# A decoder layer on Trainium2: the last expert taken out of the normalisation of all tokens, its tokens normalised by slots and scattered

## Chip, core and metric

The kernel runs on one core of one Trainium2 chip. The metric is the device time of one execution in microseconds; lower is better. Before the change it is 1770.06 us, the median of 3 runs (1768.85 to 1771.56).

## What is computed

One decoder layer over 256 tokens of width 2048, in float32: a mixer of retention and gated linear attention, cross-attention into 256 memory tokens, and a mixture of 32 experts of which each token takes two. Each of the three is followed by `x <- LayerNorm(alpha * x + f(x))`. The change touches only the end of the third:

```python
    hid = jax.nn.silu(xblk @ w_exp_gate[e]) * (xblk @ w_exp_up[e])
    return hid @ w_exp_down[e]
...
    h = layer_norm(DEEPNORM_ALPHA * h + ffn, ln3_g[l], ln3_b[l])
...
    y = (xf - mu) * lax.rsqrt(var + LN_EPS) * g.astype(jnp.float32) + b.astype(jnp.float32)
```

`ffn` adds, for each token, its two experts' outputs times their gates.

## The kernel before

**Experts.** Each expert has 32 slots (`CAP`). `gather` (by a 0/1 matrix on TensorE) brings the tokens of four experts into slots; `gate_up(e)` multiplies them with the expert's gate and up weights, which come in four quarters of 2 MB (`gu`, line 1082), each used by two of the eight rounds of its loop; SiLU, product and transposes give `hht`; `down_all(e, hht)` multiplies with the down weights, two halves of 2 MB (`dp`, line 1120). One expert's output is 32 slots x 2048 values; in PSUM it stands as 128 partitions x 512, four column blocks of 512 under each other. `combine` brings the outputs of four experts back to the tokens: a matmul with the transposed, gate-weighted slot matrix `GT` (line 1513) and an addition into `fo` (line 1515), the sum `alpha * h + ffn` of all 256 tokens, in two halves of 128 tokens.

**Order of the work.** Each engine runs its instructions in the order in which the code is written. Small background steps (generators in `bgq`) are put between the rounds of `gate_up` by `step()`: `combine`, and for the last LayerNorm `bg_gb3` (line 1461, put in at expert 29), which loads gamma and beta of `ln3` as rows (`raw3`, line 1468), splits them into `row3` for a matmul of 6 rows, and spreads gamma and beta over all partitions (`gb3`, line 1482, from `row_bcast`, line 1446).

**Transfers.** All weights are loaded by SyncE (SP) in one queue, in the order of use, each as soon as its buffer is free: gate/up quarters and other large tiles share one pool of 8 buffers, the down halves a pool of 3. SP's transfers report to eight semaphores, `DMAHW0` to `DMAHW7`, in turn; a transfer waits until the one eight places ahead of it has landed.

**The last expert (31).** Its down weights are stored apart (`w_last`), cut by columns (`LASTC`: three blocks of 512 columns and two of 256). For each block `down(i)` multiplies, ScalarE copies the slots out (`ys`, line 1624), and `finish(i - 1)` brings the block before to all tokens (line 1631), adds it (1632), takes the block's statistics (`bn_stats`, 1635), and GpSimd multiplies it by gamma (1638). Then `ln_rstd` (841 to 843) gives mean and 1/std, lines 1649 to 1657 turn them into `nbT`, and each block of 512 columns is finished by a matmul of 6 rows and one VectorE instruction (1674, 1675) and stored (1660); the last 512 columns go another way (1664 to 1669).

Of the kernel before, what the change touches and what calls it, by code (L numbers as in the profile page):

```python
# [36 lines left out]
MOX = [0, 0, 1, 0, 0, 1, 9, 9]  # L37


LASTC = [(0, 512), (512, 512), (1024, 512), (1536, 256), (1792, 256)]  # L40


def bcast_rows(ap1d, n, off=0, parts=128):
# [4 lines left out]
def layer(ctx: ExitStack, tc: tile.TileContext, a, out):  # L48
# [1075 lines left out]
    lastw = []  # L1124

    def dn_cols(c0, n):

        def load():
            if c0 % 1024 == 0:
                lastw.append(qq[0].tile([128, 4 * 1024], F32, name="dl", tag="q"))  # L1130
            c = c0 % 1024
            t = lastw[-1][:, 4 * c:4 * c + 4 * n]
            sp.dma_start(out=t, in_=a["w_last"][:, 4 * c0:4 * c0 + 4 * n])
            t = t.rearrange("p (k f) -> p k f", k=4)
            return [t[:, k] for k in range(4)]
        return xpiece(load, "q", int(c0 % 1024 == 0))
# [324 lines left out]

    def bg_gb3():
        g_, r_ = pair([128, 2, D], name="gb3"), pair([6, 2, D], name="raw3")
        gb3.extend(g_[:, i] for i in range(2))
        raw, hi, r3 = r_[:, 0], r_[:, 1].bitcast(F32R), single([6, D], F32R, name="row3")
        gb3.append(r3)
        for i, k, n in ((0, 4, "ln3_g"), (4, 2, "ln3_b")):
            sp.dma_start(out=raw[i:i + k], in_=bcast_rows(a[n][0], D, parts=k))
        yield True

        odd = s1("odd", (6, 4))
        oi = odd[:, 0:1].bitcast(I32)
        dve.tensor_scalar(oi, pi[:6, 1, 0:1], 1, None, op0=OP.bitwise_and)
        dve.tensor_copy(odd[:, 1:2], oi)
        dve.tensor_scalar(odd[:, 2:3], odd[:, 1:2], -2.0, 1.0, op0=OP.mult, op1=OP.add)
        act.activation(hi, raw, AF.Copy)  # L1476
        act.activation(raw, raw, AF.Copy, scale=odd[:, 1:2])
        dve.scalar_tensor_tensor(r3, hi.bitcast(F32), odd[:, 2:3], raw, op0=OP.mult, op1=OP.add)
        yield True
        for c in range(4):  # L1480
            for i in range(2):
                act.activation(gb3[i][:, c * 512:c * 512 + 512], row_bcast(2 + i, c), AF.Copy)
            yield True


# [122 lines left out]
    drain()  # L1608


    g3, b3, row3 = gb3
    yq = {}
    nbr = s1("nbr", (128, 2, 6))
    pool.memset(nbr, 1.0)

    def down(i):
        c0, n = LASTC[i]
        py = acc_ps([128, n])
        k = 0
        for w in xtake(dn_ids[i]):  # L1620
            mm(py[32 * k:32 * k + 32], hht[:, 32 * k:32 * k + 32], w, start=True, stop=True)  # L1621
            k += 1
        yq[i] = s2("ys", (128, n))
        act.activation(yq[i], py, AF.Copy)

    def finish(i):
        c0, n = LASTC[i]
        sl = slice(c0, c0 + n)
        for t in range(2):
            p = aux_ps([128, n])  # L1630
            mm(p, GT[(LAST,)][:, t * 128:(t + 1) * 128], yq[i], start=True, stop=True)  # L1631
            dve.tensor_tensor(fo[t][:, sl], fo[t][:, sl], p, op=OP.add)  # L1632
        for t in range(2):
            for c in range(c0, c0 + n, 256):
                dve.bn_stats(lnst[:, t, c // 256], fo[t][:, c:c + 256])  # L1635
        if n == 512:
            for t in range(2):
                pool.tensor_tensor(fo[t][:, sl], fo[t][:, sl], g3[:, sl], op=OP.mult)

    down(0)  # L1640
    for i in range(1, len(LASTC)):
        down(i)
        if i == 4:
            act.activation(lnrs[:, :, 0], lnrs[:, :, 0], AF.Sqrt)
        finish(i - 1)
    finish(len(LASTC) - 1)
    assert xs["loaded"] == len(xpieces)
# [11 lines left out]
    def store(t, sl):
        sp.dma_start(out=out[0, t * 128:(t + 1) * 128, sl], in_=fo[t][:, sl])  # L1660

    sl = slice(1536, D)
    d = fo[1][:, sl]
    act.activation(d, d, AF.Identity, scale=lnrs[:, 1, 1:2], bias=nb[:, 1:2])
    pool.tensor_tensor(d, d, g3[:, sl], op=OP.mult)
    pool.tensor_tensor(d, d, b3[:, sl], op=OP.add)
    d = fo[0][:, sl]
    dve.scalar_tensor_tensor(d, d, lnmv[:, 0, 0:1], g3[:, sl], op0=OP.subtract, op1=OP.mult)
    dve.scalar_tensor_tensor(d, d, lnrs[:, 0, 1:2], b3[:, sl], op0=OP.mult, op1=OP.add)
# [28 lines left out]
def _layout(inputs):  # L1698

    gate, up = (inputs[n][0].reshape(NE, 4, 4, 128, 512) for n in ("w_exp_gate", "w_exp_up"))  # L1700
    last = inputs["w_exp_down"][0][NE - 1].reshape(128, 4, D)
    return {
        "x_T": _rows(inputs["x"][0].T, 0, T, 0, 16).reshape(128, 16, T),
        "mem_T": _rows(inputs["mem"][0].T, 0, T, 0, 16).reshape(128, 16, T),
        "w_gl": _rows(inputs["w_in"][0], 7168, 16, 0, 16).reshape(128, 16, 16),
        "w_last": np.concatenate([last[:, :, c:c + n].reshape(128, 4 * n) for c, n in LASTC], axis=1),
        "w_gu": np.stack([up, gate], axis=2).transpose(0, 1, 4, 2, 3, 5).reshape(NE, 4, 128, 4096),
        "w_dense": np.empty((ND, 128, 1024), np.float32),
    }
# [23 lines left out]
```

## Time and profile before

| | us |
|---|---|
| median of 3 runs | 1770.06 |
| the profiled execution | 1768.08 |
| its span, first to last instruction | 1766.2 |
| TensorE busy | 1486.6 (84%) |
| VectorE, ScalarE, GpSimd busy | 639.9, 546.2, 58.9 |
| mean granted TensorE clock | 0.921 |
| read from HBM | 554.86 MB |

The page divides the span into 40 slices of 44 us. In the first half TensorE is busy in nine tenths or more and the DMA engines in five to eight tenths; from the 23rd slice (about 970 us) the DMA engines are at nine tenths or more, which is the stage of the experts. The views of the trace put every instruction in order of time; a float32 matmul stands there as two records.

### The profile page before, as it was taken

What the parts mean: (1) busy time and instruction counts of PE and PEld (TensorE: products, weight loads), DVE (VectorE), ACT (ScalarE), POOL (GpSimd) and SP (SyncE); (2) the same over time, 40 slices, a digit from 0 to 9 for tenths busy, and PEclk for the clock granted to TensorE, in tenths of its full rate; (3) what the DMA queues carried; (4) which work ended last, traced back from release to release, by engine and by line L of the source; (5) the groups of instructions that cost most, each with busy time, mean ns of one, the idle gap of its engine ahead of it and who ended that gap; (6) DMA issues with size and microseconds to landing.
All of it is one profiled execution on the core that took longest, in us unless ns stands there. A gap on an engine that the chain in (4) does not pass through costs nothing. (4 is left out here: it accounts for less than half of the span.)

```text
span 1766.2 us, 25332 instructions
## 1 busy us (share of the span) xinstructions
PE 1486.6 (84%) x10828; PEld 1000.3 (57%) x10828; DVE 639.9 (36%) x981; ACT 546.2 (31%) x830; POOL 58.9 (3%) x56
## 2 busy tenths in 40 slices
PE   9999999999999999999986776677577657675667
PEld 7788888888888889889542322323123223231332
DVE  6575665665445767555231010010010100100105
ACT  6545444554443565443320201111102011111031
POOL 0000110000000041000000000000000000000002
PEclk9999999999999999999988878887888888888978
DMA  8554555655567655686999999999999999999996
GB/s 266 165 180 155 170 169 201 224 169 189 195 206 218 199 171 180 234 321 252 412 429 429 431 429 432 430 430 430 430 431 430 431 430 430 430 430 432 429 389 248
DMA packets 81665, 558.67 MB, mean 316 GB/s; under 512 B 15046, under 2 KB 15430, under 8 KB 57094
## 3 DMA queue, kind: packets, MB, share of 16 engines
q1 hardware_dynamic: 81548, 556.99, 80.5%
q8 instruction: 87, 1.43, 0.3%
q14 instruction: 30, 0.25, 0.0%
HBM read 554.86 MB, written 2.10 MB: 315 GB/s over the span
## 5 line engine op out<-in xcount | busy, mean ns | idle before, releaser
L1555 PE MATMUL acc<-gu,yz 128*32 128x256 f32 x3584 | 286.9, 466 | 153.8 <-DMA gu<-in_w_gu 148.8
L154 DVE TENSOR_TENSOR wl<-wr,wh 128x1024 fp32r<-128x1024 f32 x271 | 334.8, 1249 | 155.3 <-ACT wh L153 140.8
L153 ACT ACTIVATE wh<-wr 128x1024 fp32r<-128x1024 f32 x271 | 281.8, 1056 | 173.7 <-DMA wr<-in_w_dense 92.3
L1555 PEld LDWEIGHTS acc<-gu,yz 128*32 128x32 f32 x3584 | 118.3, 126 | 330.8 <-DMA gu<-in_w_gu 207.8
L1586 PE MATMUL acc<-dp,eht 128*32 128x512 f32 x944 | 148.0, 758 | 67.8 <-DMA dp<-in_w_exp_down 61.5
L1571 DVE TENSOR_TENSOR ehh<-acc,ehh 64x256 f32<-64x256 f32 x32 | 13.3, 416 | 427.3 <-ACT ehh L1570 427.3
L1592 ACT ACTIVATE yz<-acc 32x512 f32<-32x512 f32 x124 | 72.9, 588 | 208.3 <-PE acc L1586 207.2
L1570 ACT ACTIVATE ehh<-acc 64x256 f32<-64x256 f32 x32 | 12.2, 380 | 363.5 <-PE acc L1555 363.5
L1586 PEld LDWEIGHTS acc<-dp,eht 128*32 128x32 f32 x944 | 30.1, 125 | 154.3 <-DMA dp<-in_w_exp_down 78.1
L1515 DVE TENSOR_TENSOR fo<-fo,aux 128x512 f32<-128x512 f32 x64 | 44.0, 687 | 174.1 <-PE aux L1513 174.1
L208 PE MATMUL acc<-wh,xT 128*128 128x512 f32 x256 | 101.5, 397 | 0.0
L210 PE MATMUL acc<-wh,xT 128*128 128x512 f32 x256 | 99.8, 390 | 0.0
L209 PE MATMUL acc<-wl,xT 128*128 128x512 f32 x256 | 99.7, 389 | 0.0
L229 PE MATMUL acc<-xT,wh 128*128 128x512 f32 x384 | 97.8, 399 | 1.5 <-ACT wh L153 1.2
L229 PEld LDWEIGHTS acc<-xT,wh 128*128 128x128 f32 x384 | 70.2, 190 | 15.5 <-ACT wh L153 1.4
L1316 PEld LDWEIGHTS aux<-P,h 128*128 128x128 f32 x512 | 59.9, 192 | 15.9 <-issue 15.8
L1322 DVE TENSOR_SCALAR yz<-aux,lnT 128x128 f32<-128x128 f32 x56 | 19.1, 403 | 133.8 <-PE aux L1316 133.8
L1513 PE MATMUL aux<-yz,GT 128*128 128x512 f32 (+1 forms) x128 | 66.7, 647 | 0.0
L1316 PE MATMUL aux<-P,h 128*128 128x128 f32 x512 | 66.5, 282 | 0.0
L229 PE MATMUL acc<-h1T,wh 128*128 128x512 f32 x256 | 63.9, 394 | 0.0
L229 PE MATMUL acc<-memT,wh 128*128 128x512 f32 x256 | 63.8, 394 | 0.0
L208 PEld LDWEIGHTS acc<-wh,xT 128*128 128x128 f32 x256 | 48.0, 188 | 10.9 <-issue 1.1
(392 smaller groups left out, 2024.8 us busy)
## 6 DMA issues: line engine op xcount, KB each, us to landing
gu<-in_w_gu SPq DMA_DIRECT2D x127, 2048.0 KB, 27.0
wr<-in_w_dense SPq DMA_DIRECT2D x271, 512.0 KB, 3.4
dp<-in_w_exp_down SPq DMA_DIRECT2D x59, 2048.0 KB, 31.1
dn<-in_w_exp_down SPq DMA_DIRECT2D x8, 512.0 KB, 3.9
dl<-in_w_last SPq DMA_DIRECT2D x3, 1024.0 KB, 28.8
mtok<-in_mem_T SPq DMA_DIRECT2D x2, 1024.0 KB, 6.7
xr<-in_x SPq DMA_DIRECT2D x4, 512.0 KB, 4.3
gu<-in_w_gu SPq DMA_DIRECT2D x4, 512.0 KB, 9.7
```

The lines of the kernel that those rows point to most:

```text
L153: act.activation(hi, raw, AF.Copy)
L154: dve.tensor_tensor(lo, raw, hi.bitcast(F32), op=OP.subtract)
L208: mm(accs[t], xh, hi[:, kc], start=(K == 0), stop=False)
L209: mm(accs[t], xh, lo[:, kc], start=False, stop=False)
L210: mm(accs[t], xl, hi[:, kc], start=False, stop=(K == 15))
L229: mm(accs[f].rearrange("p (a b) -> p a b", a=2), wf, xt, start=(q + kc == 0), stop=(q + kc == 6))
L1316: mm(p[:, k], h2[t][:, (m * q + k) * 128:(m * q + k + 1) * 128], P[:, t], start=(t == 0), stop=(t == 1))
L1513: mm(p, GT[es][:m, t * 128:(t + 1) * 128], y[:m, c * 512:(c + 1) * 512], start=True, stop=True)
L1515: dve.tensor_tensor(d, d, p, op=OP.add)
L1555: mm(pg[32 * j:32 * j + 32].rearrange("p (f c) -> p f c", c=2), xe[e][:, kc], w[:, :, 2 * (j % 2):2 * (j % 2) + 2], start=(kc == 0), stop= ...
L1586: mm(py[32 * j:32 * j + 32], hht[:, 32 * k:32 * k + 32], w, start=(k == 0), stop=(k == 3))
L1592: act.activation(ys[e // GB][32 * (e % GB):32 * (e % GB) + 32, 512 * j:512 * j + 512], py[32 * j:32 * j + 32], AF.Copy)
```

## The change

All tokens' sums are taken without expert 31. While expert 31's gate and up weights come in, the statistics of `fo` are taken (`last_stats`), GpSimd multiplies `fo` by gamma, and the values of expert 31's tokens are copied by a 0/1 matrix into slots (`last_slots`: `z`, 128 partitions x 512, four partitions for a slot). All 256 tokens are normalised and stored as if expert 31 gave nothing. Its down product is added in slots, `z` is normalised there, and one indirect transfer of GpSimd writes the slots over the rows of these tokens; an empty slot has an index beyond the output and is skipped. Expert 31's down weights are loaded in two halves as those of the other experts.

```diff
@@ bg_gb3
-        gb3.extend(g_[:, i] for i in range(2))
+        gb3.extend((g_[:, 0], g_[:, 1, 0:512], g_[:, 1, 512:1024]))
...
+        for i, n in ((1, "ln3_g"), (2, "ln3_b")):
+            for j in range(4):
+                sp.dma_start(out=gb3[i][32 * j:32 * j + 32], in_=bcast_rows(a[n][0], 512, off=512 * j, parts=32))
...
-            for i in range(2):
-                act.activation(gb3[i][:, c * 512:c * 512 + 512], row_bcast(2 + i, c), AF.Copy)
+            act.activation(gb3[0][:, c * 512:c * 512 + 512], row_bcast(2, c), AF.Copy)
@@ new
+    def last_slots():
+        O, G = s1("Og", (128, 2, 4, CAP)), s1("Pg", (128, 2, 4, CAP))
+        for t in range(2):
+            dve.tensor_scalar(O[:, t], io4, rk1[:, t, LAST:], None, op0=OP.is_equal)
+            dve.tensor_scalar(G[:, t], io4, rk1[:, t, LAST:], W[:, t, LAST:], op0=OP.is_equal, op1=OP.mult)
...
+        for t in range(2):
+            mm(pq[:, 0:2], flat(O, t), tk[:, t], start=(t == 0), stop=(t == 1))
+        for t in range(2):
+            mm(pq[:, 2:3], flat(G, t), ones[:, 0:1], start=(t == 0), stop=(t == 1))
+        sv = s1("sv", (128, 4))
+        act.activation(sv[:, 0:3], pq[:, 0:3], AF.Copy)
...
+        for t in range(2):
+            for j in range(4):
+                mm(pz[32 * j:32 * j + 32], O[:, t, 0], fo[t][:, 512 * j:512 * j + 512], start=(t == 0), stop=(t == 1))
+        z = lst["z"] = s2("z", (128, 512))
+        act.activation(z, pz, AF.Copy)
+        yield True
+
+    def last_stats():
+        for t in range(2):
+            for c in range(4):
+                for k in range(2):
+                    dve.bn_stats(lnst[:, t, 2 * c + k], fo[t][:, 512 * c + 256 * k:512 * c + 256 * k + 256])
+                sl = slice(512 * c, 512 * c + 512)
+                pool.tensor_tensor(fo[t][:, sl], fo[t][:, sl], gb3[0][:, sl], op=OP.mult)
@@ gate_up
-            bgq.append(slots((LAST,)))
+            bgq.extend((last_slots(), last_stats()))
...
             if e == LAST and q < 4:
                 step()
+                step()
@@ the end: down, finish, store and the loops over them are taken out
-    g3, b3, row3 = gb3
+    g3, gc, bc3, row3 = gb3
     nbr = s1("nbr", (128, 2, 6))
     pool.memset(nbr, 1.0)
...
     ln_rstd(8)
...
+    def base(t, c):
         sl = slice(c * 512, (c + 1) * 512)
+        p = aux_ps([128, 512])
         mm(p, nbT[:, t * 128:(t + 1) * 128], row3[:, sl], start=True, stop=True)
         dve.scalar_tensor_tensor(fo[t][:, sl], fo[t][:, sl], lnrs[:, t, 1:2], p, op0=OP.mult, op1=OP.add)
+        sp.dma_start(out=out[0, t * 128:(t + 1) * 128, sl], in_=fo[t][:, sl])
+
+    for c in range(4):
+        base(0, c)
+    py = acc_ps()
+    n = 0
+    for i in eids[LAST][1]:
+        for w in xtake(i):
+            k, j = divmod(n, 4)
+            mm(py[32 * j:32 * j + 32], hht[:, 32 * k:32 * k + 32], w, start=(k == 0), stop=(k == 3))
+            n += 1
...
+    dve.scalar_tensor_tensor(z, py, lst["gate"], z, op0=OP.mult, op1=OP.add)
+    st = s1("lst", (128, 12))
+    for k in range(2):
+        dve.bn_stats(st[:, 6 * k:6 * k + 6], z[:, 256 * k:256 * k + 256])
+
+    pst = acc_ps([128, 4, 12])
+    for j in range(4):
+        mm(pst[:, j], lst["id4"][:, j].rearrange("p a b -> p (a b)"), st, start=True, stop=True)
+    base(1, 0)
+    sa = s1("lsa", (128, 4, 12))
+    dve.tensor_copy(sa, pst)
+    mv = s1("lmv", (128, 4))
+    dve.bn_aggr(mv[:, 0:2], sa.rearrange("p a b -> p (a b)"))
+    act.activation(mv[:, 2:3], mv[:, 1:2], AF.Sqrt, bias=eps_t)
+    dve.scalar_tensor_tensor(z, z, mv[:, 0:1], gc, op0=OP.subtract, op1=OP.mult)
+    dve.reciprocal(mv[:, 3:4], mv[:, 2:3])
+    dve.scalar_tensor_tensor(z, z, mv[:, 3:4], bc3, op0=OP.mult, op1=OP.add)
+    for c in range(1, 4):
+        base(1, c)
+    pool.indirect_dma_start(out=out[0].rearrange("t (j f) -> (t j) f", j=4),
+                            out_offset=bass.IndirectOffsetOnAxis(ap=lst["idx"][:, 0:1], axis=0),
+                            in_=z, in_offset=None, bounds_check=4 * T - 1, oob_is_err=False)
```

**Where instructions move.** First SP's queue at `bg_gb3`, between expert 29's down weights (`dp`) and expert 30's gate/up weights (`gu`), with the semaphores each transfer waits for. Before:

```order
L1120 DMA dp<-in_w_exp_down 128x4096 [waits DMAHW5_49,DMAHW4_49,PE_49]
L1468 DMA raw_11685<-in_ln_g 4x2048
L1468 DMA raw_11685<-in_ln_b 2x2048 [waits DMAHW6_49]
L1082 DMA gu<-in_w_gu 128x4096 [waits DMAHW7_49,PE_49]
L1082 DMA gu<-in_w_gu 128x4096 [waits DMAHW5_49,DMAHW6_49,DMAHW0_49,DVE_49]
```

Now:

```order
L1119 DMA dp<-in_w_exp_down 128x4096 [waits DMAHW5_49,DMAHW4_49,PE_49]
L1453 DMA raw_11685<-in_ln_g 4x2048
L1453 DMA raw_11685<-in_ln_b 2x2048 [waits DMAHW6_49]
L1456 DMA gb_11684<-in_ln_g 32x512 [waits DMAHW7_49,PE_49]
L1456 DMA gb_11684<-in_ln_g 32x512 [waits DMAHW0_49]
L1456 DMA gb_11684<-in_ln_g 32x512 [waits DMAHW1_49]
L1456 DMA gb_11684<-in_ln_g 32x512 [waits DMAHW2_49]
L1456 DMA gb_11684<-in_ln_b 32x512 [waits DMAHW3_49]
L1456 DMA gb_11684<-in_ln_b 32x512 [waits DMAHW4_49]
L1456 DMA gb_11684<-in_ln_b 32x512 [waits DMAHW5_49]
L1456 DMA gb_11684<-in_ln_b 32x512 [waits DMAHW6_49]
L1081 DMA gu<-in_w_gu 128x4096 [waits DMAHW7_49,PE_49]
```

Eight small transfers now stand ahead of expert 30's first quarter, one on each semaphore, and that quarter's `DMAHW7` is now that of the first of them.

Second, TensorE from expert 31's first quarter to the end of its gate-up (`gu`, `yz`: its matmuls; `Pg`, `GT`: the slot matrix of experts 28 to 30 and its transpose). Before:

```order
L1555 MATMUL acc<-gu,yz 32x256 x8
L1501 MATMUL aux<-ident,Pg 96x128 x2
L1555 MATMUL acc<-gu,yz 32x256 x8
L1513 MATMUL aux<-yz,GT 128x512 x4
L1555 MATMUL acc<-gu,yz 32x256 x8
L1513 MATMUL aux<-yz,GT 128x512 x4
L1555 MATMUL acc<-gu,yz 32x256 x16
L1501 MATMUL aux<-ident,Pg 128x128 x2
L1555 MATMUL acc<-gu,yz 32x256 x24
```

Now:

```order
L1594 MATMUL acc<-gu,yz 32x256 x8
L1488 MATMUL aux<-ident,Pg 96x128 x2
L1500 MATMUL aux<-yz,GT 128x512 x2
L1594 MATMUL acc<-gu,yz 32x256 x8
L1500 MATMUL aux<-yz,GT 128x512 x6
L1594 MATMUL acc<-gu,yz 32x256 x8
L1531 MATMUL aux<-tk,Og 128x2 x2
L1533 MATMUL aux<-ones,Pg 128x1 x2
L1594 MATMUL acc<-gu,yz 32x256 x8
L1545 MATMUL acc<-fo,Og 32x512 x8
L1594 MATMUL acc<-gu,yz 32x256 x32
```

The combining of experts 28 to 30 is closed up ahead of the second quarter, and four small products and the eight of `z` (L1545) come between.

Third, GpSimd's end. Before:

```order
L1614 MEMSET nbr 128x12
L1638 TENSOR_TENSOR fo<-fo,gb_11684 128x512 x6
L1665 TENSOR_TENSOR fo<-fo,gb_11684 128x512
L1666 TENSOR_TENSOR fo<-fo,gb_11684 128x512
L1726 UNCONDITIONAL_BRANCH
```

Now:

```order
L1521 IOTA tk 128x1 x2
L1523 MEMSET tk 128x2
L1526 MEMSET off 32x1 x4
L1556 TENSOR_TENSOR fo<-fo,gb_11684 128x512 x8
L1653 MEMSET nbr 128x12
L1702 DMA out<-z,idx 1024x512
```

All eight blocks are multiplied by gamma on GpSimd, the clearing of `nbr` stands behind them instead of ahead, and the indirect transfer is last.

## Rows read from the trace of the kernel before

**Rows 1.** The page: span and instructions, DMA share in 40 slices (tenths).

```profile
span 1766.2 us, 25332 instructions
...
DMA  8554555655567655686999999999999999999996
```

**Rows 2.** Stretches: us, busy of PE, PEld, DVE, ACT, POOL; granted clock, DMA share, GB/s.

```profile
1675.00:1680.00 5.00, 0.00 (x0) 0.00 (x0) 0.00 (x0) 0.86 (x1) 0.00 (x0) 0.66 1.01 426
1680.00:1685.00 5.00, 1.24 (x6) 1.24 (x7) 1.88 (x1) 4.94 (x6) 0.00 (x0) 0.50 0.62 267
1685.00:1690.00 5.00, 5.00 (x31) 3.49 (x31) 0.46 (x1) 1.37 (x3) 0.11 (x1) 0.50 0.86 338
...
1742.00:1744.00 2.00, 2.00 (x11) 0.35 (x9) 1.50 (x3) 0.00 (x0) 0.00 (x0) 1.00 0.50 203
...
1755.00:1760.00 5.00, 3.69 (x8) 1.81 (x8) 4.45 (x8) 1.08 (x2) 2.54 (x2) 0.51 0.42 152
```

**Rows 3.** SP's issues in order of time: start, us, line, transfer.

```profile
1663.56 0.36 SPq L1082 DMA_DIRECT2D gu<-in_w_gu  x1
1685.48 0.35 SPq L1082 DMA_DIRECT2D gu<-in_w_gu  x1
...
1700.43 0.33 SPq L1120 DMA_DIRECT2D dp<-in_w_exp_down  x1
...
1715.12 0.33 SPq L1133 DMA_DIRECT2D dl<-in_w_last  x1
1719.95 0.33 SPq L1133 DMA_DIRECT2D dl<-in_w_last  x1
```

**Rows 4.** Issue to landing (us, last column), windows at 1655, 1663, 1685, 1700, 1757, 1761.

```profile
dp<-in_w_exp_down SPq DMA_DIRECT2D x1, 2048.0 KB, 29.7
...
gu<-in_w_gu SPq DMA_DIRECT2D x1, 2048.0 KB, 26.0
...
gu<-in_w_gu SPq DMA_DIRECT2D x1, 2048.0 KB, 8.9
...
dp<-in_w_exp_down SPq DMA_DIRECT2D x1, 2048.0 KB, 14.7
...
out<-fo SPq DMA_DIRECT2D x1, 256.0 KB, 2.5
...
out<-fo SPq DMA_DIRECT2D x2, 256.0 KB, 3.6
```

**Rows 5.** Timeline, experts 29 to 31 and the end: start, us, instruction, idle before.

```profile
1660.18 3.30 PE L1555 MATMUL acc<-gu,yz 128*32 128x256 f32 x32 [2.93 <-DMA gu<-in_w_gu]
...
1698.44 1.92 PE L1586 MATMUL acc<-dp,eht 128*32 128x512 f32 x16 [0.37 <-ACT eht L1577]
...
1719.98 1.11 PE L1555 MATMUL acc<-gu,yz 128*32 128x256 f32 x16 [2.91 <-DMA gu<-in_w_gu]
...
1732.24 2.03 PE L1555 MATMUL acc<-gu,yz 128*32 128x256 f32 x32
...
1743.80 1.40 DVE L1635 BATCH_NORM_STATS2 lnst<-fo 128x6 f32<-128x256 f32 x4
...
1754.61 0.21 ACT L1651 ACTIVATE nbr<-nb 128x4 fp32r<-128x4 f32 x1 [0.49 <-DVE nb L1649]
...
1756.08 3.15 PE L1674 MATMUL acc<-row,nbT 6*128 6x512 f32 x6 [0.46 <-ACT nbT L1657]
...
1760.27 0.74 DVE L1675 SCALAR_TENSOR_TENSOR fo<-fo,lnrs,acc 128x512 f32<-128x512 f32 x1
```

**Rows 6.** Groups by line and shape, 1700 to 1767 us; last row 1640 to 1700.

```profile
L1638 POOL TENSOR_TENSOR fo<-fo,gb 128x512 f32<-128x512 f32 x6 | 7.5, 1270 | 59.4 <-DVE lnst L1635 59.4
L1495 DVE TENSOR_SCALAR Pg<-io,rk,W 128x128 f32<-128x128 f32 x2 | 0.6, 341 | 0.0
L1446 PE MATMUL aux<-lnrow,ident 64*128 64x128 f32 x64 | 11.7, 353 | 11.5 <-ACT gb L1482 11.5
```

**Rows 7.** The same view as rows 6, GpSimd over the whole span.

```profile
L992 POOL TENSOR_TENSOR v<-vm,v 128x512 fp32r<-128x512 f32 x8 | 15.4, 1947 | 367.6 <-ACT v L991 367.6
```

More of the change, by code (lines that the diff above doesn't have):

```diff
@@ L37 @@
 MOX = [0, 0, 1, 0, 0, 1, 9, 9]
-LASTC = [(0, 512), (512, 512), (1024, 512), (1536, 256), (1792, 256)]
 def bcast_rows(ap1d, n, off=0, parts=128):
@@ L1122, in dn_pair @@
         return xpiece(load, kind, 1)
[L1124 to L1136, printed above, removed]
     g0 = [gu_piece(0, q) for q in range(4)]
@@ L1149, in layer @@
         gu = [gu_piece(e, q) for q in range(4)]
-        eids[e] = gu, [dn_cols(c0, n) for c0, n in LASTC] if e == NE - 1 else [dn_pair(e, i) for i in range(2)]
+        eids[e] = gu, [dn_pair(e, i) for i in range(2)]
     lim["p"] = 2
@@ L1519, in layer @@
     LAST = NE - 1
+    lst = {}
+    def last_slots():
[3 more added lines that the diff above has]
+            dve.tensor_scalar(G[:, t], io4, rk1[:, t, LAST:], W[:, t, LAST:], op0=OP.is_equal, op1=OP.mult)
+        id4 = lst["id4"] = s2("id4", (128, 4, 4, 32))
+        for k in range(4):
+            act.activation(id4[:, :, k], ident.rearrange("p (a b) -> p a b", a=4), AF.Copy)
+        tk = s1("tk", (128, 2, 2))
+        for t in range(2):
+            pool.iota(tk[:, t, 0:1], pattern=[[0, 1]], base=512 * t, channel_multiplier=4,
+                      allow_small_or_imprecise_dtypes=True)
+        pool.memset(tk[:, :, 1], 1.0)
+        off = s1("off", (128, 4))
+        for j in range(4):
+            pool.memset(off[32 * j:32 * j + 32, 0:1], 4.0 * T + j)
+        yield True
+        pq = aux_ps([128, 4])
+        flat = lambda x, t: x[:, t].rearrange("p a b -> p (a b)")
+        for t in range(2):
[4 more added lines that the diff above has]
+        act.activation(sv[:, 0:3], pq[:, 0:3], AF.Copy)
+        idx = s1("idx", (128, 4), I32)
+        dve.scalar_tensor_tensor(off[:, 1:2], sv[:, 1:2], -4.0 * T, off[:, 0:1], op0=OP.mult, op1=OP.add)
+        dve.tensor_tensor(off[:, 1:2], off[:, 1:2], sv[:, 0:1], op=OP.add)
+        dve.tensor_copy(idx[:, 0:1], off[:, 1:2])
+        lst.update(gate=sv[:, 2:3], idx=idx)
+        yield True
+        pz = acc_ps()
+        for t in range(2):
[3 more added lines that the diff above has]
+        act.activation(z, pz, AF.Copy)
+        yield True
@@ L1521, in gate_up @@
+    def last_stats():
+        for t in range(2):
+            for c in range(4):
[3 more added lines that the diff above has]
+                pool.tensor_tensor(fo[t][:, sl], fo[t][:, sl], gb3[0][:, sl], op=OP.mult)
+                if c % 2:
+                    yield True
     def gate_up(e):
@@ L1608, in layer @@
     drain()
-    g3, b3, row3 = gb3
-    yq = {}
+    g3, gc, bc3, row3 = gb3
     nbr = s1("nbr", (128, 2, 6))
     pool.memset(nbr, 1.0)
[L1616 to L1647, printed above, removed]
     ln_rstd(8)
@@ L1657, in layer @@
     act.activation(nbT, pn, AF.Copy)
[L1659 to L1669, printed above, removed]
@@ new lines, in layer @@
+    for c in range(4):
[7 more added lines that the diff above has]
+            n += 1
+    assert xs["loaded"] == len(xpieces)
+    z = lst["z"]
+    dve.scalar_tensor_tensor(z, py, lst["gate"], z, op0=OP.mult, op1=OP.add)
+    st = s1("lst", (128, 12))
+    for k in range(2):
+        dve.bn_stats(st[:, 6 * k:6 * k + 6], z[:, 256 * k:256 * k + 256])
@@ new lines, in layer @@
+    pst = acc_ps([128, 4, 12])
+    for j in range(4):
+        mm(pst[:, j], lst["id4"][:, j].rearrange("p a b -> p (a b)"), st, start=True, stop=True)
[7 more added lines that the diff above has]
+    dve.reciprocal(mv[:, 3:4], mv[:, 2:3])
@@ L1700, in _layout @@
     gate, up = (inputs[n][0].reshape(NE, 4, 4, 128, 512) for n in ("w_exp_gate", "w_exp_up"))
-    last = inputs["w_exp_down"][0][NE - 1].reshape(128, 4, D)
     return {
@@ L1705, in _layout @@
         "w_gl": _rows(inputs["w_in"][0], 7168, 16, 0, 16).reshape(128, 16, 16),
-        "w_last": np.concatenate([last[:, :, c:c + n].reshape(128, 4 * n) for c, n in LASTC], axis=1),
         "w_gu": np.stack([up, gate], axis=2).transpose(0, 1, 4, 2, 3, 5).reshape(NE, 4, 128, 4096),
```

6 lines of the change are left out of this document (removed).

## The prediction

> **What bounds the kernel now.** I read the page first. Its row of DMA shares stands at nine tenths or more from the 23rd of 40 slices on [rows 1], so in the stage of the experts the weights set the pace. The stretches show how that ends. At 1675 to 1680 the engines move 426 GB/s and TensorE does nothing; the next two stretches of 5 us move only 267 and 338 GB/s; at 1742 to 1744 the rate has fallen to 203 [rows 2]: the last weights are in at about 1743, and the last 23 us of the 1766.2 us span [rows 1] hold no weight at all. A step here counts only if it delays the weights, or lies in the chain between the last weights and the end.
>
> SP's issues and landings give the rule of the queue. Expert 30's second down half is issued at 1700.43 and lands 14.7 us later, at 1715.13; the transfer eight places behind it (the first of the last expert's down weights) is issued at 1715.12. The next one goes at 1719.95, and expert 31's first matmul, which needs the quarter eight places ahead of that, starts at 1719.98 [rows 3 to 5]. So each transfer waits for the landing eight places ahead, as the semaphores in the listed order say. The drop to 267 GB/s is such a wait: expert 30's second quarter stands eight places behind transfers that landed earlier but also needs the buffer of gamma and beta's rows, and is issued only at 1685.48, 21.9 us after the first at 1663.56 [rows 3]. Against 426 GB/s the two slow stretches lose 5 x (159 + 88) / 426 = 2.9 us.
>
> **1. The stream of weights.** Added are eight loads of 64 KB, 0.5 MB together, 1.2 us at 426 GB/s. Their place matters more. Expert 29's second down half is issued at about 1655.0 and lands after 29.7 us, at 1684.7 [rows 4]. The sixth of the eight waits for that landing, and so do all that stand behind it, expert 30's first quarter included. That quarter goes out at about 1685.7 in place of 1663.56. It meets empty queues, so it should land faster than the 8.9 us of the quarter issued at 1685.48 [rows 4]: 6.8 us, an estimate, 4.9 us of bytes (2 MB at 426 GB/s) and 1.9 of start-up. That is 1692.5. Six transfers on, at 4.9 us each, expert 31's first quarter lands at 1722.0; it was 1719.98 [rows 5]. I take **+2.0**. Bounds: 0, if the hole of before, which lies at the same time, costs as much as the new one; and with 8.9 in place of 6.8 for the first quarter 1724.1, or +4. What would turn the sign is in the third rival.
>
> **2. Gamma and beta spread by loads.** Eight of the sixteen products with their copies (L1446, L1482) go, and with them TensorE's 11.5 us halt on ScalarE [rows 6]. I cost that at nothing: the halt lies where TensorE would otherwise wait for expert 30's weights, which are not there before 1692. If they were, its worth is in the third rival.
>
> **3. Expert 31's gate-up.** Before, 12.3 us lie between its first matmul and the block at 1732.24 [rows 5]; these hold the combining of experts 28 to 30. Now that is closed up ahead of the second quarter: 12.3 less half a quarter that moves behind it (1.0, by 2.03 for 32 records) plus a wait for the copy of the slot matrix that no matmul covers (0.5) is 11.8. Then half a quarter, 1.0; four VectorE instructions that TensorE must wait for at 0.34 each (the 341 ns row [rows 6]), 1.4; another half quarter, 1.0; and the eight products of `z`, 1.92 as the 16 records of that shape at 1698.44 [rows 5]. Parts overlap by 1.1. So from 1722.0 the first gamma multiplication of GpSimd can start at 1722.0 + 11.8 + 1.0 + 1.4 + 1.0 + 1.9 - 1.1 = **1738.0**. Gate-up itself ends near 1743, covered by what follows.
>
> **4. GpSimd.** Eight multiplications at 1.27 us [rows 6] are 10.2 us: 1748.2. The clearing of `nbr` now stands behind them (0.1), and ScalarE's write into `nbr` waits for it: **1748.3**. Before, six ran between the blocks of the last expert, and the clearing was done long ahead.
>
> **5. To the first base block.** From ScalarE's `nbr` to the first product of six rows there are 1756.08 - 1754.61 = 1.47 us [rows 5], so 1749.8. The down products of expert 31 stand behind four of these on TensorE, which I put at 0.8 for the first and 0.4 for each further one when full, less overlap: 1751.6. Then 32 records of 512 columns. At the higher level they take 2 x 1.92 = 3.8 us [rows 5]. But TensorE has been idle for some 5 us ahead, and the stretch at 1755 to 1760, which follows an idle stretch of 4 us in the tail of before, has a granted clock of 0.51, the 1.2 GHz level [rows 2]; there they would take 7.7. I take 5.3, between the ends, since a block of 32 records that began after idling took 3.30 against 2.03 for one at speed [rows 5], a factor of 1.6 at most, and some of it returns on the way: down is done at **1756.9**.
>
> **6. The slots' own LayerNorm**, all in a row: the product with the gate 0.74 (the nearest VectorE row of 512 columns [rows 5]), two statistics at 0.35 from 1.40 for four, 0.7; four small products, 1.1 (eight records between 0.10 each, as in 3.30 for 32, and 0.353, the mean at the low clock [rows 5, 6]); the product and VectorE instruction of `base(1, 0)`, which stands ahead, 1.2; copy, aggregation and reciprocal 0.7 (0.2 to 0.3 each, as the small instruction at 1754.61); two instructions on `z`, 1.5; the last three blocks at 0.7, 2.1; gaps 0.4. That is 8.4: VectorE ends at **1765.3**, against 1761.0 before [rows 5].
>
> **7. Store and scatter.** The last store lands 2.5 to 3.6 us after its issue [rows 4]; I take 3.1: 1768.4. The indirect transfer waits for all eight stores, since it writes over them. No row shows one: below, a 256 KB store at 2.5; above, 8.9, a loaded 2 MB transfer [rows 4]. I take 3.5, the store with 1 us for GpSimd's own part, as it is nearest to a store of that size into an idle queue: 1771.9. The end stands 1.2 us behind the last landing before (1761.4 + 3.6 = 1765.0, span 1766.2), and so again: 1773.2.
>
> A rule of the Trainium skill (*DMA: Bandwidth & Descriptors*, section "Anatomy of one DMA — SWDGE (gpsimd) path") gives a transfer issued by GpSimd a fixed cost of about 2.0 us and its bytes at 436 GB/s: 2.6 us for 256 KB, an estimate, and the sum would be 0.9 lower. The trace has no transfer of GpSimd to hold against it.
>
> **Sum.** Removed are the 18 us from the last weights to the last VectorE instruction (1743 to 1761); put in their place are 1738.0 to 1765.3. 1773.2 - 1766.2 = **+7.0 us**. The profiled execution took 1768.08, 2.0 below the median; on the median 1770.06 + 7.0 = **1777.0**. A measurement of this kernel tells about 0.2% (3.5 us) from no change.
>
> **Rivals.**
>
> *GpSimd slower still.* Its other multiplications took 1.95 us each [rows 7], and these run while VectorE takes statistics. The six of before ran beside VectorE too and took 1.27. If not: 8 x 0.68 = +5.4, 1782.4. Chance 0.06.
>
> *The terms fall at their low ends.* No delay of the stream (-2.0), the higher clock in the down products (-1.5), a scatter at 2.5 (-1.0): 1772.5, no change to tell. Chance 0.15.
>
> *The other side: the weights stay the bound and the hole goes.* TensorE's 11.5 us halt is gone, so nothing keeps the buffer of gamma's rows and expert 30's quarters could follow at once. Then the 2.9 us of hole are won, the weights end near 1741, and GpSimd starts early enough to be done before the last down half. The end is 1741.2 + 1.9 for the last half's products + 8.4 + 3.1 + 3.5 + 1.2 = 1759.3, 6.9 below 1766.2: 1763.2. It decides whether expert 30's first quarter is issued near 1669 instead of 1685, and whether the eighth multiplication ends before about 1739. Against it stand the semaphores in SP's order and 10.2 us of multiplications that cannot begin before expert 31's second quarter. Chance 0.08.
>
> The forecast itself, that what is taken off TensorE (the last expert's way to all tokens) returns on GpSimd, in `z` and in the scatter: 0.71.
>
> **Range.** Low 1770.0 takes in most of the second rival; high 1783.5 takes in the first and a scatter at its upper bound with the other terms as they are (1777.0 + 5.4 = 1782.4). Faster 0.09, within 0.2% 0.15, slower 0.76.
>
> **What would show it.** Expert 30's first quarter issued at about 1685.7, after the landing of expert 29's second down half; expert 31's first matmul at about 1722; eight multiplications in a row on GpSimd from about 1738, and ScalarE's `nbr` waiting for POOL; a granted clock near 0.5 around the last down products, at 5 us or more; the scatter issued only after the last store's landing and 2.5 us or more long. I am wrong if weights land before 1720, if `nbr` waits for VectorE instead, or if the scatter overlaps the stores.

## The result, and the profile after

The changed kernel takes 1778.73 us, the median of five (1778.41 to 1781.24); the kernel before took 1769.18 beside it. The ratio is 1.0063, 95% interval 1.0051 to 1.0075: 9.5 us slower where 7 were forecast. The profiled execution took 1778.59 with a span of 1776.9, 10.7 longer than before.

The page of the changed kernel, its span and the DMA shares in 40 slices:

```profile
span 1776.9 us, 25287 instructions
...
DMA  8554556655566555687999999999999999999894
```

Before, the row had nines from its 20th slice (not from the 23rd, as I had counted) up to the last but one [rows 1]. Now there is an eight in the third slice from the end: the stream of weights has a hole. Stretches of 5 us, in the columns of [rows 2], and SP's issues around them:

```profile
1675.00:1680.00 5.00, 1.08 (x20) 0.35 (x12) 0.00 (x0) 1.45 (x1) 0.00 (x0) 1.00 0.61 233
1680.00:1685.00 5.00, 0.00 (x0) 0.00 (x0) 2.34 (x1) 4.91 (x7) 0.07 (x1) 0.54 0.42 170
1685.00:1690.00 5.00, 4.14 (x22) 1.31 (x26) 0.42 (x1) 0.28 (x1) 0.29 (x4) 0.50 0.77 226
```

```profile
1662.80 11.53 SPq L1456 DMA_DIRECT2D gb<-in_ln_g  x4
1679.65 6.18 SPq L1456 DMA_DIRECT2D gb<-in_ln_b  x4
1685.94 2.15 SPq L1081 DMA_DIRECT2D gu<-in_w_gu  x4
```

Against 426 GB/s these stretches lose 5 x (193 + 256 + 200) / 426 = 7.6 us, where before they lost 2.9. The eight small loads take SP from 1662.8 to 1685.8, and expert 30's first quarter leaves at 1685.94 instead of 1663.56 [rows 3].

The timeline of the end: start, us, instruction, idle time before it and its releaser.

```profile
1724.15 1.41 PE L1594 MATMUL acc<-gu,yz 128*32 128x256 f32 x16 [3.10 <-DMA gu<-in_w_gu]
1726.62 3.78 PE L1500 MATMUL aux<-yz,GT 96*128 96x512 f32 x4 [0.47 <-ACT GT L1490]
...
1741.74 9.94 POOL L1556 TENSOR_TENSOR fo<-fo,gb 128x512 f32<-128x512 f32 x8 [56.34 <-PE acc L1545]
...
1751.77 0.21 ACT L1657 ACTIVATE nbr<-nb 128x4 fp32r<-128x4 f32 x1 [2.31 <-POOL nbr L1653]
1753.27 2.07 PE L1668 MATMUL aux<-row,nbT 6*128 6x512 f32 x4 [0.46 <-ACT nbT L1663]
1755.27 5.43 PE L1679 MATMUL acc<-dp,eht 128*32 128x512 f32 x32
1760.78 0.75 DVE L1683 SCALAR_TENSOR_TENSOR z<-acc,sv,z 128x512 f32<-128x512 f32 x1 [3.95 <-PE acc L1679]
1766.73 2.06 DVE L1669 SCALAR_TENSOR_TENSOR fo<-fo,lnrs,aux 128x512 f32<-128x512 f32 x3
1772.77 1.19 POOL L1702 DMA_INDIRECT out<-z,idx  x1 [21.03 <-issue]
```

The rows stand on one path, each ahead of the next. Before, VectorE was done at 1761.0 [rows 5], now at 1768.79, and behind it stand a store and a scatter. The step by step comparison with the forecast is below; first what the runs show of each cause.

### The profile page after: what moved, and what is told of

Read it like the earlier page. It is cut to its first block, busy times and chain, and to the rows that moved or that the text cites. A ratio compares the mean times of both kernels' runs of the same rounds, so it can differ in the third digit from the quotient of the medians.

```text
span 1776.9 us, 25287 instructions
## 1 busy us (share of the span) xinstructions
PE 1473.9 (83%) x10800; PEld 991.0 (56%) x10800; DVE 638.8 (36%) x984; ACT 541.4 (30%) x825; POOL 61.1 (3%) x64
## 5 line engine op out<-in xcount | busy, mean ns | idle before, releaser
L1500 PE MATMUL aux<-yz,GT 128*128 128x512 f32 (+1 forms) x128 | 71.5, 689 | 0.5 <-ACT GT L1490 0.5
```

The source lines that it names most:

```text
L1500: mm(p, GT[es][:m, t * 128:(t + 1) * 128], y[:m, c * 512:(c + 1) * 512], start=True, stop=True)
```

## Experiments

Each is an edit of the changed kernel, timed against the kernel before on the same chip. The ratios come from several executions, the rows and the span of a run from a single one, and executions of one kernel differ by 2 to 6.5 us; so a gain in the time is read from the ratio.

**The place of the eight loads.** `late_bcast` issues them behind the last weights:

```diff
@@ bg_gb3, taken out
-                sp.dma_start(out=gb3[i][32 * j:32 * j + 32], in_=bcast_rows(a[n][0], 512, off=512 * j, parts=32))
@@ behind hht = gate_up(LAST)
+            sp.dma_start(out=gb3[i][32 * j:32 * j + 32], in_=bcast_rows(a[n][0], 512, off=512 * j, parts=32))
```

> The changed kernel with the eight 64 KB loads of gamma and beta issued behind expert 31's down weights; bytes, buffers and all else as in the change. Theory A (the loads delay the weights by their place: the sixth waits for expert 29's second down half, and expert 30's first quarter stands behind it): expert 30's first quarter is issued near 1663 again, expert 31's first matmul starts 4 to 5 us earlier than 1724.15, and the span falls from 1776.9 to about 1772. Rival B (the hole comes from the buffer that gamma's rows hold, and the eight loads cost their bytes only): the first matmul moves by no more than 1.2 us and the span stays at 1775.7 or above.

Measured: ratio 1.0038 (1.0025 to 1.0050) against the change's 1.0063 (1.0051 to 1.0075), some 4.4 us; the span of the profiled execution, the fastest of six, is 1769.6. Its stretches and timeline:

```profile
1675.00:1680.00 5.00, 5.00 (x30) 3.49 (x30) 0.00 (x0) 0.43 (x1) 0.00 (x0) 0.50 1.02 433
1680.00:1685.00 5.00, 3.97 (x35) 1.69 (x34) 1.45 (x1) 4.94 (x6) 0.26 (x3) 0.64 1.01 431
1685.00:1690.00 5.00, 3.12 (x18) 1.01 (x22) 1.30 (x2) 1.26 (x4) 0.37 (x4) 0.70 1.00 426
```

```profile
1662.99 23.25 SPq L1081 DMA_DIRECT2D gu<-in_w_gu  x4
1719.50 1.11 PE L1591 MATMUL acc<-gu,yz 128*32 128x256 f32 x16 [1.43 <-DMA gu<-in_w_gu]
1721.43 1.98 PE L1497 MATMUL aux<-yz,GT 96*128 96x512 f32 x4 [0.47 <-ACT GT L1487]
1734.18 9.93 POOL L1553 TENSOR_TENSOR fo<-fo,gb 128x512 f32<-128x512 f32 x8 [47.75 <-PE acc L1542]
```

The first quarter leaves at 1662.99 again, expert 31 starts 4.65 us earlier, and there is no hole at all, not even the one of before. So theory A holds. The third rival's mechanism is seen too: this run has neither TensorE's halt of before nor its hole (that the one made the other was not tried by itself). But expert 31 starts only 0.5 us ahead of the 1719.98 of before [rows 5], so little of that gain reaches it. Nor do the last weights come earlier than before: the last down half is issued at 1712.69 and lands 32.0 us later, near 1744.7, where the stream of before ends at about 1743. Without a hole the stream runs out slowly. At 1740 to 1745 the first row is of this run, the second of the change:

```profile
1740.00:1745.00 5.00, 0.35 (x2) 0.09 (x2) 1.15 (x3) 2.03 (x4) 4.16 (x5) 0.66 0.51 194
1740.00:1745.00 5.00, 5.00 (x80) 2.39 (x76) 4.93 (x18) 0.60 (x1) 3.26 (x3) 1.00 1.02 433
```

two_loads (149 GB/s) and combo3 (168) run out in the same way; why, no run tests.

The span fell by 2.6 us more than the start of expert 31: from there to GpSimd's first multiplication it is 14.7 us here and 17.6 in the change, with the same instructions. That is not the work of the loads: combo2 and combo3 below have them at the same place and take 17.5. I come back to that.

**Places or bytes.** `two_loads` loads the same 0.5 MB at the old place in two transfers:

```diff
-            for j in range(4):
-                sp.dma_start(out=gb3[i][32 * j:32 * j + 32], in_=bcast_rows(a[n][0], 512, off=512 * j, parts=32))
+            sp.dma_start(out=gb3[i], in_=bcast_rows(a[n][0], 512))
```

> The changed kernel with the eight loads of 64 KB replaced, at the same place in SP's queue, by two of 256 KB: the same bytes, but all four quarters of gamma and beta are those of the first 512 columns, so the slots' rows are normalised with wrong factors. Theory A (it is the number of places in the queue, each waiting for the landing eight ahead): expert 30's first quarter then waits only for a quarter of expert 29 and is issued near 1670, not 1686, the rate stays near 430 GB/s from 1675 to 1690 or nearly so, and expert 31's first matmul starts 4 us or more before 1724.15; span about 1771. Rival B (the bytes or the broadcast reads at this place): first matmul and span as in the change, within 1 us.

Measured: ratio 1.0038 (1.0025 to 1.0050), span 1773.7.

```profile
1666.15 0.35 SPq L1455 DMA_DIRECT2D gb<-in_ln_b  x1
1671.55 14.44 SPq L1081 DMA_DIRECT2D gu<-in_w_gu  x4
1720.91 1.55 PE L1593 MATMUL acc<-gu,yz 128*32 128x256 f32 x16 [2.93 <-DMA gu<-in_w_gu]
```

The quarter leaves at 1671.55, and the rate stays at 416 to 430 GB/s from 1675 to 1690. Expert 31 starts 3.2 us earlier, a little less than the 4 asked for, and the span is 1773.7 for about 1771; the rest of theory A is as expected. It is mostly the number of places, each bound to the landing eight ahead: the same bytes in two places cost 1.4 us against late_bcast's 1719.50, in eight places 4.65. These differences are good to a microsecond or two only, since the executions differ ahead of the loads already. Expert 29's first product, in the change, late_bcast and two_loads:

```profile
1659.48 3.28 PE L1594 MATMUL acc<-gu,yz 128*32 128x256 f32 x32 [2.93 <-DMA gu<-in_w_gu]
1660.89 2.05 PE L1591 MATMUL acc<-gu,yz 128*32 128x256 f32 x32 [1.34 <-DMA gu<-in_w_gu]
1661.34 2.03 PE L1593 MATMUL acc<-gu,yz 128*32 128x256 f32 x32 [2.92 <-DMA gu<-in_w_gu]
```

Counted from there, eight places cost 6.1 us and two 1.0. The ratio of two_loads is that of late_bcast.

**The scatter.** `no_scatter` leaves it out.

```diff
-    pool.indirect_dma_start(out=out[0].rearrange("t (j f) -> (t j) f", j=4),
...
```

> The changed kernel without the indirect transfer: the rows of expert 31's tokens keep the values without that expert. Theory A (the transfer waits for the last store and stands wholly in the path): the span ends 1.2 us after the last store's landing at about 1771.6, so 1772.8, 4.1 us less than 1776.9. Rival B (most of the end is the program's own closing, which the transfer overlaps): the span falls by 2 us or less.

Measured: ratio 1.0041 (1.0026 to 1.0055). The header of its views and VectorE's last row:

```profile
core 0 of [0], span 1773.6 us
...
1767.45 2.06 DVE L1669 SCALAR_TENSOR_TENSOR fo<-fo,lnrs,aux 128x512 f32<-128x512 f32 x3
```

From VectorE's end to the end of the span it takes 1773.6 - 1769.5 = 4.1 us, in the change 1776.9 - 1768.8 = 8.1. The scatter costs 4.0 us, all of it in the path; the ratios differ by 0.22%, 3.9 us, but their intervals touch.

**The order on TensorE.** `down_first` puts the loop of expert 31's down products ahead of `nbr`'s transposes and the base blocks; VectorE's order stays.

```diff
@@ ahead of g3, gc, bc3, row3 = gb3
+            mm(py[32 * j:32 * j + 32], hht[:, 32 * k:32 * k + 32], w, start=(k == 0), stop=(k == 3))
@@ behind base(0, c), taken out
-            mm(py[32 * j:32 * j + 32], hht[:, 32 * k:32 * k + 32], w, start=(k == 0), stop=(k == 3))
```

> The changed kernel with expert 31's down products ahead of nbr's transposes and the base blocks on TensorE; VectorE's order as it is. Theory A (the down products ran at the low level only because TensorE had idled for 5 us, and the slots' chain starts late because they stand behind the base blocks): they start at about 1748, right behind the transposes of hht, take 3.8 to 4 us instead of 5.43 at a granted clock near 1, and the chain of z starts when the four base blocks on VectorE are done, near 1757 instead of 1760.8: span about 1773. Rival B (the down products are slow of themselves, by their weights or because the last weights land late): they take over 5 us wherever they stand, or start after 1750, and the span falls by under 2 us.

Measured: ratio 1.0049 (1.0032 to 1.0066), span 1772.9. The products and the chain of `z` moved as theory A said.

```profile
1746.25 1.92 PE L1656 MATMUL acc<-dp,eht 128*32 128x512 f32 x16 [0.43 <-ACT eht L1617]
1749.70 1.92 PE L1656 MATMUL acc<-dp,eht 128*32 128x512 f32 x16 [1.53 <-DMA dp<-in_w_exp_down]
1755.57 0.74 DVE L1683 SCALAR_TENSOR_TENSOR z<-acc,sv,z 128x512 f32<-128x512 f32 x1
```

The same 32 records take 3.84 us behind a busy TensorE; in the change they took 5.43, soon after TensorE had stood idle for 4.75. The granted clock is 1.00 at 1745 to 1750 here; in the change:

```profile
1755.00:1760.00 5.00, 5.00 (x29) 1.24 (x32) 1.82 (x3) 0.00 (x0) 0.00 (x0) 0.61 0.65 211
```

The chain of `z` starts at 1755.57 instead of 1760.78. That the span met its forecast was in part luck: from expert 31's first product to GpSimd's first multiplication, ahead of what was moved, it took 14.7 us here and 17.6 in the change. From that multiplication to the end it is 32.8 us in place of 35.2, so the new order won 2.4; in the time the intervals overlap.

**Who holds up `nbr`.** `memset_first` clears `nbr` ahead of GpSimd's multiplications.

```diff
@@ last_stats
+        nbr = lst["nbr"] = s1("nbr", (128, 2, 6))
+        pool.memset(nbr, 1.0)
         for t in range(2):
```

> The changed kernel with the clearing of nbr ahead of GpSimd's eight multiplications instead of behind. Theory A (GpSimd's queue sets when the rows for the base blocks are made): ScalarE's nbr starts behind VectorE's nb at about 1750.5 instead of 1751.77, and all that follows moves by the same 1.3 us: span about 1775.6. Rival B (something else ends last there, such as the multiplied blocks themselves): span within 0.3 us of 1776.9.

Measured: ratio 1.0073 (1.0056 to 1.0090), span 1777.2: nothing won in the time, as rival B said, but for another reason than the blocks.

```profile
1742.32 9.94 POOL L1558 TENSOR_TENSOR fo<-fo,gb 128x512 f32<-128x512 f32 x8 [2.24 <-PE acc L1545]
1750.31 0.75 DVE L1656 SCALAR_TENSOR_TENSOR nb<-lnmv,lnrs 128x2 f32<-128x2 f32 x1
1751.15 0.21 ACT L1658 ACTIVATE nbr<-nb 128x4 fp32r<-128x4 f32 x1 [1.07 <-DVE nb L1656]
1751.39 0.89 DVE L1659 TENSOR_TENSOR nbr<-nb,nbr 128x4 f32<-128x4 f32 x1 [0.33 <-ACT nbr L1658]
```

ScalarE's `nbr` now follows VectorE's `nb`. But `nb` takes 0.75 us and `nbr` 0.89, two instructions of a few values each that in the profile of before stand at 0.16; `nbr` ends at 1752.28, with GpSimd's last multiplication at 1752.26. From GpSimd's first multiplication to the first base product it is 11.07 us here and 11.53 in the change, so 0.5 of the 1.3 us was won. VectorE was held while GpSimd multiplied, not by the order of a queue; in the change too `nb` took 0.78, hidden behind the clearing. The Trainium skill (*SBUF — State Buffer*, section "SBUF: two separate sides") has a port pair that VectorE and GpSimd share, locked for a whole instruction, taken by a VectorE instruction with two inputs in SBUF and by one in a two-port mode; the two rows agree. Two runs test it by instructions with one input, the second with a single value in each:

```diff
-    dve.scalar_tensor_tensor(nb, lnmv[:, :, 0], -1.0, lnrs[:, :, 1], op0=OP.mult, op1=OP.mult)
+    for t in range(2):
+        dve.tensor_scalar(nb[:, t:t + 1], lnmv[:, t, 0:1], lnrs[:, t, 1:2], -1.0, op0=OP.mult, op1=OP.mult)
@@ memset_one_input; in memset_one_value four, nbr[:, t, 2 + k:3 + k]
-    dve.tensor_tensor(nbr[:, :, 2:4], nb2, nbr[:, :, 0:2], op=OP.subtract)
+        dve.tensor_scalar(nbr[:, t, 2:4], nbr[:, t, 0:2], -1.0, nb[:, t:t + 1], op0=OP.mult, op1=OP.add)
```

> The run with the clearing of nbr first, and nb and nbr's second half worked out by VectorE instructions with one input in place of those with two. Theory A (a VectorE instruction with two inputs in SBUF does not run beside a GpSimd multiplication but ends with it: nb took 0.75 and nbr 0.89 us there against 0.16 before): each of the new ones takes 0.2 us or less, nbr is done near 1751.3 in that run's time instead of 1752.28, and the span falls by about 1 us. Rival B (the waits come from the order of semaphores, not from the inputs): nbr ends with GpSimd's last multiplication again, and nothing is won.

> As the run with one-input instructions (nbr cleared first), but nbr's second half by four VectorE instructions of one value per partition in place of two of two values; there the one-value instructions (nb) took 0.17 us each while GpSimd multiplied, the two of two values 1.42 together, ending with GpSimd's last multiplication. Theory A (an instruction of one input and an even number of values also takes the port that it shares with GpSimd, one of a single value does not): the four take 0.7 us together, nbr is done 0.6 us before GpSimd's last multiplication ends, and nbT's transposes start then. Rival B (VectorE waits for GpSimd's last block in any case): the four end with that multiplication again.

Measured: ratios 1.0060 (1.0043 to 1.0076) and 1.0068 (1.0053 to 1.0083). VectorE's rows of the first:

```profile
1750.35 0.17 DVE L842 RECIPROCAL lnrs<-lnrs 128x2 f32<-128x2 f32 x1 [2.01 <-ACT lnrs L841]
1750.55 0.34 DVE L1657 TENSOR_SCALAR nb<-lnmv,lnrs 128x1 f32<-128x1 f32 x2
1751.22 1.42 DVE L1661 TENSOR_SCALAR nbr<-nbr,nb 128x2 f32<-128x2 f32 x2 [0.33 <-ACT nbr L1659]
```

and GpSimd's and VectorE's of the second:

```profile
1746.75 7.43 POOL L1558 TENSOR_TENSOR fo<-fo,gb 128x512 f32<-128x512 f32 x6
1752.23 0.34 DVE L1657 TENSOR_SCALAR nb<-lnmv,lnrs 128x1 f32<-128x1 f32 x2
1752.90 0.57 DVE L1662 TENSOR_SCALAR nbr<-nbr,nb 128x1 f32<-128x1 f32 x4 [0.33 <-ACT nbr L1659]
```

The instructions of one value ran at 0.17 beside GpSimd. Those of two values took 1.42: the first of them 1.29, to the end of GpSimd's last multiplication, the second less than 0.25 behind it. There my expectation for one input failed. Nor does the number of values decide alone: `RECIPROCAL`, with one input and two values, took 0.17 while GpSimd multiplied. What sets the two apart was not tried. The four of the last run ended at 1753.47, 0.7 us ahead of GpSimd's end at 1754.18. That is too little to be seen in the times.

**The clock at expert 31's start.** In the change four records of the combining take 3.78 us, in the profile of late_bcast 1.98. `fill_idle` puts five products that nobody reads ahead of expert 31's first quarter:

```diff
@@ gate_up, ahead of its rounds
+        if e == LAST:
+            pw = aux_ps([128, 512])
+            for i in range(5):
+                mm(pw[:, 0:256], ident, gb3[0][:, 0:256], start=True, stop=True)
```

> The changed kernel with five products of 256 columns on TensorE ahead of expert 31's first quarter, in the time in which it waited for that quarter; nobody reads them. Theory A (from expert 31's first product to GpSimd's first multiplication the change took 17.6 us, where the run with late loads took 14.7 with the same instructions, because TensorE had idled for 3.1 us before it and its first products of the combining ran at the 1.2 GHz level, 3.78 us for four records against 1.98): with the wait filled they run at the higher level, the distance is 15 us, and the span falls by some 2.5 us. Rival B (the low level comes from the kind of products or from the experts' stage as a whole): four records take 3.7 us again and the distance stays above 17 us.

Measured: ratio 1.0049 (1.0033 to 1.0064), span 1777.7.

```profile
1726.65 1.11 PE L1598 MATMUL acc<-gu,yz 128*32 128x256 f32 x16
1728.58 1.98 PE L1500 MATMUL aux<-yz,GT 96*128 96x512 f32 x4 [0.47 <-ACT GT L1490]
1741.32 9.91 POOL L1556 TENSOR_TENSOR fo<-fo,gb 128x512 f32<-128x512 f32 x8 [56.11 <-PE acc L1545]
```

The granted clock in that stretch, in the change and in this run:

```profile
1725.00:1730.00 5.00, 4.53 (x14) 1.40 (x6) 0.69 (x1) 1.17 (x5) 0.00 (x0) 0.50 0.99 426
1725.00:1730.00 5.00, 4.53 (x30) 2.45 (x28) 0.25 (x1) 2.15 (x7) 0.00 (x0) 0.98 1.03 439
```

The four records take 1.98, and the distance is 14.7 us: theory A. So it is TensorE's idle time, but not the wait for that quarter alone: memset_first's four records took 3.78 behind a wait of 1.21 us, down_first's 1.98 behind 1.28. The span of this one execution did not fall, for its expert 31 started at 1726.65, 2.5 us later than in the change, and its down products took 5.83. Of the 2.5 us, 1.5 were there when expert 30's first quarter was issued (1687.48); the rest may be the five products' own, which ran from 1723.49 right up to expert 31's first product. The intervals of the ratios overlap, so the gain in the time is not shown.

**Put together.** `combo1` has the late loads, `nbr` first with one input, and down products, `z`'s sum and statistics ahead of the base blocks. `combo2` moves the rest of `z`'s LayerNorm behind all base blocks, `combo3` has `nbr` by single values and two base products ahead of the products of the statistics, `combo4` the five products besides.

```diff
@@ combo3, behind z's bn_stats
+    base(0, 0)
+    base(0, 1)
     pst = acc_ps([128, 4, 12])
     for j in range(4):
         mm(pst[:, j], lst["id4"][:, j].rearrange("p a b -> p (a b)"), st, start=True, stop=True)
...
+    base(0, 2)
+    base(0, 3)
+    for c in range(4):
+        base(1, c)
     sa = s1("lsa", (128, 4, 12))
```

> The loads behind the weights, nbr cleared first and worked out with one input, the down products and the slots' sum and statistics ahead of the base blocks, the rest of the slots' LayerNorm between the base blocks. Theory A (stream 5 us, down products earlier and at the high level, VectorE filled): down products at 3.8 us right behind gate-up, last VectorE instruction near 1754 where the last weights' time is that of the run with late loads, last store landed 3 us later and 4 us for the scatter: span about 1762, device time about 1764 to 1766, faster than before (1768 to 1770). Rival B (VectorE becomes the bound, or the stores queue up): span 1766 or more.

> As combo1, but all eight base blocks ahead of the last steps of the slots' LayerNorm, so that the stores land while VectorE ends those steps. Theory A (the scatter's wait is for the last store's landing, and it needs the slots only then): the last store goes out 2.3 us earlier than in combo1 and the scatter starts some 2 us earlier: span about 1760. Rival B (the scatter then waits for the slots as long as it did for the store): within 0.7 us of combo1.

> As combo2, with nbr by instructions of one value, and the first two base products on TensorE ahead of the four small products of the slots' statistics. Theory A (in combo2 VectorE stood 1.72 us still before the first base block, since the base products waited behind products that wait for VectorE's statistics): the first base block on VectorE follows the statistics at once, and last store, slots and scatter move 1.5 us earlier: span about 1762.5, device time about 1764, faster than before by some 0.25%. Rival B (the base products wait for nbT or for the multiplied blocks, not for their place): VectorE's idle time before the first base block stays over 1 us, and the time is that of combo2.

> As combo3, with the same five products ahead of expert 31's first quarter. Theory A: the distance from expert 31's first product to GpSimd's first multiplication falls from 17.5 to about 15 us, span about 1760 and device time about 1763. Rival B: it stays, and the time is that of combo3; or the down products at the end are then bound by the landing of the last weights and only 1 us is won.

| run | us, median | before beside it | ratio, interval | span |
|---|---|---|---|---|
| combo1 | 1767.95 | 1768.06 | 1.0002 (0.9993 to 1.0012) | 1765.4 |
| combo2 | 1765.61 | 1768.06 | 0.9988 (0.9978 to 0.9998) | 1764.1 |
| combo3 | 1765.11 | 1768.33 | 0.9982 (0.9973 to 0.9991) | 1762.2 |
| combo4 | 1764.80 | 1768.07 | 0.9983 (0.9974 to 0.9992) | 1761.9 |

VectorE's first base block in combo2 and combo3, combo3's scatter, and combo4's second half of the down products, one fence each:

```profile
1750.57 5.36 DVE L1679 SCALAR_TENSOR_TENSOR fo<-fo,lnrs,aux 128x512 f32<-128x512 f32 x8 [1.72 <-PE aux L1678]
```

```profile
1748.09 1.39 DVE L1680 SCALAR_TENSOR_TENSOR fo<-fo,lnrs,aux 128x512 f32<-128x512 f32 x2
1757.97 1.19 POOL L1707 DMA_INDIRECT out<-z,idx  x1 [11.30 <-issue]
```

```profile
1744.27 1.92 PE L1662 MATMUL acc<-dp,eht 128*32 128x512 f32 x16 [1.91 <-DMA dp<-in_w_exp_down]
```

combo1 was forecast too low by 3.4 us of span: the second half of its down products waited 2.45 us for weights and then took 3.49 in place of 1.92. combo2 won in the time (2.3 us), though its profiled execution moved by 1.3 only: there expert 31 started 2.1 us later than in combo1's, and the four records took 3.78 in place of 1.98. In combo3 the still stand of 1.72 us is gone, and the scatter goes out 1.87 us earlier than combo2's 1759.84 (0.6 of it because expert 31 started that much earlier). In combo4 the distance to GpSimd's first multiplication is 14.6 us, but the second half of the down products now waits 1.91 us for its weights, and the time is that of combo3: theory A for the distance, its second rival for the time. Those weights come out of the slow end of the stream shown at late_bcast. The ratios of combo2, combo3 and combo4 overlap, so the steps between them are seen in the rows only. So combo3, 0.18% (0.09 to 0.27) faster than the kernel before, is the version to keep.

## Why the prediction held, step by step

| step | forecast | measured |
|---|---|---|
| expert 30's first quarter issued | 1685.7 | 1685.94 |
| expert 31's first product | 1722.0 | 1724.15 |
| from there to GpSimd's first multiplication | 16.0 | 17.6 |
| from there to ScalarE's `nbr` | 10.3 | 10.0 |
| to the first base product, to the down products | 1.5, 1.8 | 1.5, 2.0 |
| down products | 5.3 | 5.43 |
| from their end to VectorE's end | 8.4 | 8.1 |
| last store | 3.1 | 2.8 |
| scatter and end | 4.7 | 5.3 |
| end of the span | 1773.2 | 1776.9 |

The 3.7 us by which the span came out longer are two terms. (The forecast's own terms add up to 1773.1.)

**The first quarter into an empty queue.** I took 6.8 us from issue to use and had 8.9 as the upper bound, from the quarter issued at 1685.48 [rows 4]. Expert 30 starts at 1694.91, 9.0 us after the issue. The bound was the better row: before too that quarter met a queue that had run low. That is 2.2 us.

**Expert 31 up to `z`.** I reckoned this stretch with durations of before, partly at the high level. In the change the low level lasted longer: the granted clock in the first and second 5 us from expert 31's first product was 0.56 and 0.75, before it was 0.66 and 1.00. That is about the 1.6 us over the forecast. TensorE's wait for the quarter does not explain it by itself, for it was 3.10 us here and 2.91 before [rows 5]; fill_idle, with products in place of the wait, has 1.00 in both. And down_first, with the same instructions as the change up to there, met the high level, so this term varies from execution to execution.

The rest came out within 0.6 us a term. The scatter measured 4.0 us by no_scatter for the 3.5 taken. From its row to its landing it is 2.8 us:

```profile
out<-fo SPq DMA_DIRECT2D x8, 256.0 KB, 2.6
out<-z,idx POOLq DMA_INDIRECT x1, 2.8
```

The Trainium skill (*DMA: Bandwidth & Descriptors*, "Anatomy of one DMA — SWDGE (gpsimd) path") gave 2.6 for 256 KB, an estimate, near this row. But only 0.08 MB were in bounds and written, for which its sum is 2.2, an estimate, below the 2.8. And the row starts 1.2 us behind the last store's landing at 1771.6, so the whole is 4.0.

One mechanism behind a right number was incomplete: I held that `nbr` waits only for GpSimd's queue. It does, and once that is mended VectorE waits for the same multiplication, so moving the clearing alone won 0.5 us of the step.

Two readings of the prediction were wrong without moving the sum. The transfer issued at 1715.12 is the fourth of the last expert's down loads, not the first; counted in the queue it is the one eight places behind. And TensorE's halt did not go, it moved: in the change TensorE stood 9.41 us, to 1685.49, ahead of expert 29's transposes, which wait for ScalarE, and ScalarE for the landing of gamma's and beta's rows at 1678.55. It cost nothing, as forecast, since expert 30's weights came at 1694.91.

Of the rivals, GpSimd did not slow down (9.94 us for eight). The third rival's mechanism, no hole once TensorE's halt is gone, was hidden by the eight loads in the queue.

## What to carry to other kernels

Where transfers share a ring of semaphores, count places in the queue, not bytes: against the same loads behind the last weights, eight of 64 KB ahead of expert 30 started expert 31 4.65 us later, two of 256 KB at that place 1.4, each good to a microsecond or two. Work taken off the busiest engine for the tail must be followed through queue order on every engine: here the down products stood behind base blocks that waited for GpSimd, and a write that overwrites stores adds its whole length behind the last of them. A stage that is worth a rewrite is worth reordering before it is given up: nearly the same instructions in another order went from 0.6% slower to 0.2% faster.

## What the runs showed of the hardware that I had not expected

A VectorE `TENSOR_SCALAR` of two values in each partition, with one input, took until GpSimd's running multiplication ended (1.29 us), while one of a single value, and a `RECIPROCAL` of two, ran beside it at 0.17 us. And an indirect transfer of some 0.08 MB that must wait for the stores costs 4.0 us of the span, more than the 2.8 from its row to its landing.
